# Chain steps in bursts and a preamble on one load queue: a change to a conv, DeltaNet and PEER block on one core

## The chip, the core and the metric

The kernel runs on one core of one Trainium2 chip. The core has a matrix engine (TensorE, PE in the rows; PEld is its weight load), three engines for elementwise work (VectorE, DVE; ScalarE, ACT; GpSimd, POOL), a queue that only issues transfers (SyncE, SP) and 16 DMA engines. Each engine runs its own instructions in the order in which they were written and waits for others by semaphores. The metric is the device time of one execution in microseconds, as the median of several runs.

## What is computed

One layer of a diffusion backbone over 256 latent and 256 context tokens of width 2048, in float32:

```python
mod  = split(silu(c)     @ w_mod + b_mod, 6)      # modulation of the latent tokens
modc = split(silu(c_ctx) @ w_mod + b_mod, 6)      # and of the context tokens
h  = rms_norm(x,   norm1_g) * (1 + mod[1])  + mod[0]
hc = rms_norm(ctx, norm1_g) * (1 + modc[1]) + modc[0]
y  = token_mixer(h, hc, ...)                      # one wide projection, then conv | gated DeltaNet
x  = x + mod[2] * y
h  = rms_norm(x, norm2_g) * (1 + mod[4]) + mod[3]
x  = x + mod[5] * peer(h, ...)                    # product keys, 16384 experts
return rms_norm(x, final_g)

# gated DeltaNet, for each of 16 heads, both directions, chunks of the 512 tokens:
#   q, k, v = l2norm/silu(short conv of 5 taps)
#   t_inv   = inverse(I + strict_lower(beta k k^T * decay))
#   scan:   v_new = u - w S;  o = (q e^g) S + attn v_new;  S = S e^g_last + k^T v_new
```

## The kernel before

The work falls into a **preamble** (to about 187 us in the trace), the **heads** (to about 1345 us) and the rest (convolution, output projections, experts), which the change doesn't touch. Instructions of every engine stand in the order in which the program writes them; no scheduler moves them.

**Products.** A weight tile of 128x2048 is loaded in two halves (`raw_load`, a ring of four buffers, all on SP's queue). `prep` splits a half into a high part `whi` (ACT, L201) and a rest `wlo` (POOL, in some places DVE, L205). `products` then runs 8 or 16 times `mm3`, which is three matmuls (L210 to L212): high by high, high by low, low by high. One `mm3` is called a product below. After each product `tick` advances a clock by one.

**Chain steps.** Everything else of a head is written as a generator that yields pauses in ticks, from the table `GAP`. `tick` runs all steps whose time has come, so their matmuls stand between two products. A head's four products are v, z (two heads late), k, q; after each follows `short_conv` (pauses C0 and C). `prepare` transposes v, k and q (pauses Pv, Pk, N), makes the Gram matrix G and A (PG, PA), and for each direction the decay matrix D, its product K with G, the high part kh, the block diagonal kb and the rest kl (PD, Pat, Pkh, Pkl). `invert` builds the inverse: a first X from kb (L706), four rounds of X and Y on compact 32-column tiles (LX, LY), then the expansion `Tf` of the result (L684) and two rounds on full tiles (F0, FX, FY, FZ), and a refinement with E, Z1, Z2. `scan` runs the recurrence over four chunks (Sv, Sr, Sn, SS, So2), normalises with So, and transposes the output (oT, Sa, Sg). PSUM banks: the products rotate through three (`psg`); the chains have two banks "d" and one each of "s", "p", "m".

**Modulation.** The first two of the six modulations are made in the preamble, in eight parts of 512 columns; a part takes eight tiles of 128x1024 (`mod_tile`, L296), a copy of the sums (`mod_row`, L312), and a transpose (`mod_columns`, L320). Between the tiles stand head 0's first products (`first_chunk`), as soon as the normalised tokens (`normed`) exist. Their sums of squares are made by `mean_squares` (ACT squares, DVE adds). Before, the tokens x and ctx are loaded in sixteen transfers that ACT issues, the modulation tiles by SP, seven in flight by three extra buffers (`mraw`). The other four modulations are made in the heads by `mods_rest`, one tile every 13 ticks.

## Time and profile before

| | us |
|---|---|
| median of 3 runs (3573.36 to 3578.66) | 3575.61 |
| the profiled execution | 3580.69 |
| its span in the profile | 3578.9 |
| PE busy | 3352.6 (94%) |
| DVE busy | 2193.8 (61%) |
| POOL busy | 1828.7 (51%) |
| ACT busy | 1485.2 (41%) |

The profile's page shows PE at nine tenths or more in most slices; the first slices and those of the heads are lower. Matmuls are pipelined, so a busy PE may still have bubbles; the distance from one start to the next tells more than a duration. A row of waits names the instruction that waited, the one that released it, the sum, the number of times and the longest.

### The profile page before, as it was taken

The numbers are of one execution on the slowest core, as the hardware profiler recorded it, in microseconds if no ns is written. First come the engines' busy times: TensorE is split into PE (matmuls) and PEld (weight loads), VectorE is DVE, ScalarE is ACT, GpSimd is POOL, SyncE is SP. The second block draws the span as 40 slices with busy tenths as digits, with TensorE's granted clock in tenths as the row PEclk, the third lists the DMA queues.
The fourth block names the chain that finished last, engine by engine and source line by source line (L and its number), as shares of the span: only waits on it lengthen the run. The fifth ranks groups of instructions, "written<-read, shape, count | busy, mean of one in ns | idle before, by whom it ended". The sixth has DMA issues, their size and how long they took to land. (4 is left out here: it accounts for less than half of the span.)

```text
span 3578.9 us, 71451 instructions
## 1 busy us (share of the span) xinstructions
PE 3352.6 (94%) x29428; PEld 3221.6 (90%) x29428; DVE 2193.8 (61%) x3963; ACT 1485.2 (41%) x2663; POOL 1828.7 (51%) x964
## 2 busy tenths in 40 slices
PE   5799999999998999999999899999999999999998
PEld 3588888888888889998999899999999999999998
DVE  3467666666667669986767999855333333333446
ACT  2234444444444444444433344544444444443443
POOL 1344434434445587777547544454454544444554
PEclk9799999999999999999999999999999999999999
DMA  8634433433432355554654456588556566665664
GB/s 308 215 119 131 127 120 120 128 125 122 131 108 81 108 181 184 183 183 153 218 183 164 144 169 211 180 318 290 195 194 196 193 194 195 194 194 191 211 210 162
DMA packets 177974, 629.26 MB, mean 176 GB/s; under 512 B 19056, under 2 KB 23792, under 8 KB 174576
## 3 DMA queue, kind: packets, MB, share of 16 engines
q1 hardware_dynamic: 174912, 618.98, 52.2%
q10 hardware_dynamic: 2736, 5.71, 0.4%
q8 instruction: 231, 3.78, 0.4%
q14 instruction: 95, 0.78, 0.1%
HBM read 601.42 MB, written 23.20 MB: 175 GB/s over the span
## 5 line engine op out<-in xcount | busy, mean ns | idle before, releaser
L205 POOL TENSOR_TENSOR wlo<-raw,whi 128x1024 fp32r<-128x1024 f32 x593 | 1447.2, 2442 | 1320.4 <-ACT whi L201 1250.2
L201 ACT CAST whi<-raw 128x1024 fp32r<-128x1024 f32 x896 | 936.6, 1048 | 1159.3 <-PE ps_p L211 779.8
L205 DVE TENSOR_TENSOR wlo<-raw,whi 128x1024 fp32r<-128x1024 f32 x303 | 429.8, 1418 | 767.0 <-ACT whi L201 764.0
L210 PE MATMUL ps_p<-hh,whi 128*128 128x256 f32 x2560 | 794.4, 310 | 11.6 <-DVE vT L559 9.1
L212 PE MATMUL ps_p<-hh,wlo 128*128 128x256 f32 x2560 | 734.6, 287 | 9.4 <-POOL wlo L205 9.3
L211 PE MATMUL ps_p<-hl,whi 128*128 128x256 f32 x2560 | 734.2, 287 | 0.0
L212 PE MATMUL ps_p<-h2h,wlo 128*128 128x256 f32 x2304 | 657.8, 286 | 18.7 <-DVE wlo L205 14.2
L210 PE MATMUL ps_p<-h2h,whi 128*128 128x256 f32 x2304 | 663.9, 288 | 3.1 <-ACT h2h L1311 1.6
L211 PE MATMUL ps_p<-h2l,whi 128*128 128x256 f32 x2304 | 656.4, 285 | 0.2 <-POOL h2l L1315 0.2
L212 PE MATMUL ps_p<-ph,wlo 128*128 128x256 f32 x2048 | 582.1, 284 | 7.2 <-POOL wlo L205 5.7
L211 PE MATMUL ps_p<-pl,whi 128*128 128x256 f32 x2048 | 580.9, 284 | 0.5 <-POOL pl L1492 0.5
L210 PE MATMUL ps_p<-ph,whi 128*128 128x256 f32 x2048 | 580.9, 284 | 0.0
L210 PEld LDWEIGHTS ps_p<-hh,whi 128*128 128x128 f32 x2560 | 499.8, 195 | 56.9 <-issue 53.7
L212 PEld LDWEIGHTS ps_p<-hh,wlo 128*128 128x128 f32 x2560 | 499.1, 195 | 11.7 <-POOL wlo L205 11.7
L211 PEld LDWEIGHTS ps_p<-hl,whi 128*128 128x128 f32 x2560 | 500.9, 196 | 0.9
L212 PEld LDWEIGHTS ps_p<-h2h,wlo 128*128 128x128 f32 x2304 | 446.1, 194 | 20.5 <-DVE wlo L205 15.4
L210 PEld LDWEIGHTS ps_p<-h2h,whi 128*128 128x128 f32 x2304 | 446.3, 194 | 3.8 <-ACT whi L201 1.9
L211 PEld LDWEIGHTS ps_p<-h2l,whi 128*128 128x128 f32 x2304 | 446.4, 194 | 0.5 <-POOL h2l L1315 0.5
L212 PEld LDWEIGHTS ps_p<-ph,wlo 128*128 128x128 f32 x2048 | 393.8, 192 | 9.9 <-POOL wlo L205 8.2
L211 PEld LDWEIGHTS ps_p<-pl,whi 128*128 128x128 f32 x2048 | 393.9, 192 | 0.7 <-POOL pl L1492 0.7
L210 PEld LDWEIGHTS ps_p<-ph,whi 128*128 128x128 f32 x2048 | 394.0, 192 | 0.2 <-issue 0.2
L911 DVE SCALAR_TENSOR_TENSOR ps_cv<-up,cw,ps_cv 128x256 f32<-128x256 f32 x464 | 226.8, 489 | 14.6
(323 smaller groups left out, 4961.7 us busy)
## 6 DMA issues: line engine op xcount, KB each, us to landing
raw<-in_w_in_dram SPq DMA_DIRECT2D x256, 512.0 KB, 4.2
raw<-in_peer_u_dram SPq DMA_DIRECT2D x256, 512.0 KB, 4.4
raw<-in_peer_v_dram SPq DMA_DIRECT2D x256, 512.0 KB, 4.5
raw<-in_w_mod_dram SPq DMA_DIRECT2D x96, 512.0 KB, 3.7
raw<-in_w_moda_dram SPq DMA_DIRECT2D x64, 512.0 KB, 5.5
raw<-in_w_dn_out_dram SPq DMA_DIRECT2D x32, 512.0 KB, 4.1
raw<-in_w_conv_out_dram SPq DMA_DIRECT2D x32, 512.0 KB, 4.6
raw<-in_w_out_dram SPq DMA_DIRECT2D x32, 512.0 KB, 4.2
```

The source lines that it names most:

```text
L201: nc.scalar.copy(hi, raw)
L205: eng.tensor_tensor(lo, raw, hi.bitcast(F32), ALU.subtract)
L210: nc.tensor.matmul(ps, wh, ah, start=start, stop=False)
L211: nc.tensor.matmul(ps, wh, al, start=False, stop=False)
L212: nc.tensor.matmul(ps, wl, ah, start=False, stop=stop)
L911: nc.vector.scalar_tensor_tensor(dst if i == CW - 1 else pr, up[n][:, :, i:i + GRID_W], cw[:, n, i:i + 1], pr, ALU.mult, ALU.add)
```

## The change

Two things. In the **preamble** the sixteen loads of x and ctx go to SP's queue, between the modulation tiles; the three extra buffers serve the first weights, which are loaded and split earlier; the constants are loaded in two pieces at the 53rd of 64 tiles into the ring of four, and copied after the seventh part; the second part's transpose comes at its sixth tile; the transposes use banks "d", and head 0's v product accumulates in bank "m", which leaves one `psg` bank free. In the **heads** `tick` runs due steps only at every third tick, the pauses are set anew, Tf is expanded in two instructions, and modulation tiles are taken in pairs at twice the pause.

```diff
-GAP = dict(N=10, C0=3, C=3.5, P0=0.5, Pv=3, Pk=4, Pn=2.5, PG=3, PA=3.5, PD=2.5, Pat=2, Pkh=2, Pkl=1, L0=4,
-           LX=4, LY=4.5, F0=7, FX=5, FY=5, FZ=2, IT=4.5, E=4, Z1=5, Z2=7, Sv=4, Sr=4, Sn=5, SS=6, So=12,
-           Sa=2, Sg=5, So2=3,
-           M=13, M0=2, DC=12, M1=16, MT=3, V=1.75, VA=2, VS=4.5, LN=4, NW=2, W=7, D=24, RT=5, RC=7, RB=11, ML=11, H0=21, HP=12, G0=4)
+GAP = dict(N=10, C0=0.5, C=3.5, P0=1.5, Pv=2.5, Pk=4, Pn=2.5, PG=3, PA=3.0, PD=2.5, Pat=2, Pkh=4.0, Pkl=1,
+           Pb=4, L0=4, LX=4, LY=4.0, F0=7, FX=5, FY=5, FZ=2, IT=6.5, E=4, Z1=5, Z2=5.0, Sv=4, Sr=5.0, Sn=5,
+           SS=5.0, So=10.5, Sa=0.5, Sg=6.5, So2=5.0, M=13.5, M0=2, DC=12, M1=16, MT=2.5, V=1.75, VA=2, VS=4.5,
+           LN=4, NW=2, W=7, D=24, RT=5, RC=7, RB=11, ML=11, H0=21, HP=12, G0=4)
...
     def tick():
         now[0] += 1
-        while todo and todo[0][0] <= now[0]:
-            step()
+        if now[0] % cur.get("burst", 1) == 0:
+            while todo and todo[0][0] <= now[0]:
+                step()
...
-        for c in range(0, NCH, 1024 // w):
-            mod_tile(ps, c, w, sc, following())
-            yield gap
+        for c in range(0, NCH, 2):
+            for k in range(2):
+                mod_tile(ps, c + k, w, sc, following.tiles.pop(0))
+            following(False)
+            yield 2 * gap
...
         for c in range(0, NCH, 2):
+            mod_load(1 if c < 14 else 0)
             for s, nm in enumerate(("ctxT", "xT")):
...
-                nc.scalar.dma_start(t, a[nm][:, c:c + 2, :])
+                nc.sync.dma_start(t, a[nm][:, c:c + 2, :])
...
-        cf = unit("cf").rearrange("p a b -> p (a b)")
-        nc.scalar.dma_start(cf, a["consts"])
...
                 x.at.append(at)
                 yield GAP['Pkl']
+            yield GAP['Pb']
...
-                nc.vector.tensor_tensor(o.rearrange("p c (b j) -> p c b j", j=32), bc(t, 2, [P, 8, 4, 32]),
-                                        bc(bd16.rearrange("p (b j) -> p b j", j=32), 1, [P, 8, 4, 32]), ALU.mult)
+                ov = o.rearrange("p c (b j) -> p c b j", j=32)
+                n = 4 if name == "Tf" else 8
+                for c in range(0, 8, n):
+                    nc.vector.tensor_tensor(ov[:, c:c + n], bc(t[:, c:c + n], 2, [P, n, 4, 32]),
+                                            bc(bd16.rearrange("p (b j) -> p b j", j=32), 1, [P, n, 4, 32]), ALU.mult)
...
-                if r == 1 and rows:
-                    mod_columns(*rows.pop(0), mod_bank)
+                if r == (5 if p == 1 else 1) and rows:
+                    mod_columns(*rows.pop(0), bank)
...
-                            pss = [psg.tile([P, len(seqs), T], F32, name="ps_p", tag="g") for _, seqs in first_jobs]
+                            pss = [mod_bank("ps_p").rearrange("p (s t) -> p s t", s=2)]
+                            pss += [psg.tile([P, len(seqs), T], F32, name="ps_p", tag="g") for _, seqs in first_jobs[1:]]
...
+                if k in (0, 1, 2, 20, 22, 24):
+                    load(len(raws) + 1)
+                if k in (11, 13, 15):
+                    prep()
+                if k == 52:
+                    cf = [raw_load(a["consts"][:, c:c + 1024], "cf") for c in (0, 1024)]
...
-            if p == 3:
+            if p == 6:
+                cur["side"] = None
                 early.close()
...
         start(mods_rest())
+        cur["burst"] = 3
         for h in range(1, nh):
```

At the program's start, PE before (ps_mod is a part's sums, x80 are ten tiles of eight matmuls, ps_modt its transpose, ps_tok and ps_rs belong to the norm):

```order
L296 MATMUL ps_mod<-raw,sc 32x128 x80
L320 MATMUL ps_modt<-cc,modrow 128x128
L296 MATMUL ps_mod<-raw,sc 32x128 x24
L339 MATMUL ps_tok<-cc,acc 128x1 x4
L296 MATMUL ps_mod<-raw,sc 32x128 x32
L352 MATMUL ps_rs<-dg,cc 128x128 x4
```

and PE after:

```order
L298 MATMUL ps_mod<-raw,sc 32x128 x80
L343 MATMUL ps_tok<-cc,acc 128x1 x4
L298 MATMUL ps_mod<-raw,sc 32x128 x32
L324 MATMUL ps_modt<-cc,modrow 128x128
L356 MATMUL ps_rs<-dg,cc 128x128 x4
```

The first transpose moved behind four more tiles, and the norm's first sums ahead of it.

At the same place, ACT before (the last loads of x and the constants, then the first square):

```order
L392 DMA x_120<-in_ctxT_dram 128x512
L392 DMA x_122<-in_xT_dram 128x512
L392 DMA x_124<-in_ctxT_dram 128x512
L392 DMA x_126<-in_xT_dram 128x512
L460 DMA cf<-in_consts_dram 128x2048
L419 ACTIVATE sq<-x_96 128x256
```

and ACT after:

```order
L271 DMA cc<-in_consts_dram 128x384
L383 ACT_TABLE_LOAD
L383 ACTIVATE cth<-pf 128x32
L420 ACTIVATE sq<-x_101 128x256
L420 ACTIVATE sq<-x_103 128x256
```

The squares now stand right behind the two small loads.

In a head, DVE around the expansion Tf before (ps_p is a short convolution's tap, Tc the compact inverse, c_749 constants; S, oacc and r belong to the scan of the head ahead):

```order
L834 SCALAR_TENSOR_TENSOR S<-S,egs,ps_S 128x128 x2
L848 SCALAR_TENSOR_TENSOR oacc<-ps_o,egs,oacc 128x128 x2
L554 SCALAR_TENSOR_TENSOR ps_p<-pad_763,pf,ps_p 128x512
L722 COPY_PREDICATED Tc<-lv,ps_Y 128x256
L684 TENSOR_TENSOR Tf<-Tc,c_749 128x1024
L690 STREAM_TRANSPOSE Tt<-Tc 128x256
L684 TENSOR_TENSOR Z<-Tt,c_749 128x1024
```

and DVE after:

```order
L830 SCALAR_TENSOR_TENSOR S<-S,egs,ps_S 128x128 x2
L546 SCALAR_TENSOR_TENSOR ps_p<-pad_1261,pf,ps_p 128x512
L718 COPY_PREDICATED Tc<-lv,ps_Y 128x256
L680 TENSOR_TENSOR Tf<-Tc,c_1246 128x512 x2
L686 STREAM_TRANSPOSE Tt<-Tc 128x256
L680 TENSOR_TENSOR Z<-Tt,c_1246 128x1024
L546 SCALAR_TENSOR_TENSOR ps_p<-pad_1261,pf,ps_p 128x512
L844 SCALAR_TENSOR_TENSOR oacc<-ps_o,egs,oacc 128x128 x2
```

Tf is two instructions, and the scan's oacc moved behind it.

In a head, PE at the Gram matrix before (ps_p are products; the step that follows is of the head ahead):

```order
L212 MATMUL ps_p<-hh_141,wlo 128x256
L637 MATMUL ps_G<-kT 128x128 x4
L210 MATMUL ps_p<-hh_140,whi 128x256
L211 MATMUL ps_p<-hl_144,whi 128x256
L212 MATMUL ps_p<-hh_140,wlo 128x256
L737 LDWEIGHTS E
```

and PE after:

```order
L212 MATMUL ps_p<-hh_153,wlo 128x256
L866 MATMUL ps_oT<-cc,oacc 128x128 x2
L629 MATMUL ps_G<-kT 128x128 x4
L210 MATMUL ps_p<-hh_151,whi 128x256
L211 MATMUL ps_p<-hl_155,whi 128x256
L212 MATMUL ps_p<-hh_151,wlo 128x256
L210 MATMUL ps_p<-hh_153,whi 128x256
L211 MATMUL ps_p<-hl_157,whi 128x256
L212 MATMUL ps_p<-hh_153,wlo 128x256
L210 MATMUL ps_p<-hh_152,whi 128x256
L211 MATMUL ps_p<-hl_156,whi 128x256
L212 MATMUL ps_p<-hh_152,wlo 128x256
```

Two steps of different heads now stand side by side, with three products behind them instead of one. Counted over the order of all heads, from the first transpose of v to the last oT, products are interrupted 614 times before and 420 times after.

## Rows read from the trace of the kernel before

**Rows 1.** Stages: stretch and length, busy us (instructions) by engine, clock, DMA share, GB/s.

```profile
0.00:187.00 187.00, 119.69 (x1477) 93.40 (x1478) 70.92 (x166) 45.45 (x98) 45.73 (x50) 0.86 0.71 253
187.00:1345.00 1158.00, 1058.56 (x10003) 965.12 (x10001) 795.14 (x1545) 493.25 (x1158) 562.62 (x346) 0.97 0.39 124
1345.00:3578.00 2233.00, 2174.32 (x17953) 2163.10 (x17951) 1327.76 (x2253) 946.50 (x1408) 1220.40 (x571) 0.99 0.59 196
```

**Rows 2.** PE's waits in the heads, 187 to 1345 us: total, times, longest.

```profile
PE ps_X L706 <- DVE kk L673: 29.0, 15, 3.5
PE ps_X L737 <- DVE Tf L684: 17.5, 13, 1.9
PE ps_qt L620 <- ACT kts L614: 8.1, 11, 0.8
PE ps_D L656 <- DVE De L669: 7.4, 8, 1.5
PE ps_vn L819 <- DVE r L810: 6.7, 12, 1.0
...
PE ps_o L841 <- DVE S L834: 4.5, 8, 1.7
```

**Rows 3.** PE's waits in the preamble, 0 to 187 us.

```profile
PE ps_modt L320 <- DVE modrow L312: 24.1, 3, 16.1
PE ps_mod L296 <- DMA raw<-in_w_moda_dram: 23.1, 22, 2.8
PE ps_p L210 <- DVE vT L559: 9.1, 1, 9.1
```

**Rows 4.** Timeline, 20 to 61 us: start, length, engine, instruction, idle before.

```profile
27.37 1.33 ACT L419 ACTIVATE sq<-x 128x256 f32<-128x256 f32 x4 [21.73 <-DMA x<-in_ctxT_dram]
...
41.17 0.28 DVE L312 COPY modrow<-ps_mod 128x128 f32<-128x128 f32 x1
...
41.51 0.48 PE L320 MATMUL ps_modt<-cc,modrow 128*128 128x128 f32 x1 [16.09 <-DVE modrow L312]
...
60.55 0.48 PE L320 MATMUL ps_modt<-cc,modrow 128*128 128x128 f32 x1 [7.56 <-DVE modrow L312]
```

**Rows 5.** Two stretches of the preamble; the last number is GB/s.

```profile
10.00:20.00 10.00, 5.67 (x88) 2.97 (x80) 0.00 (x0) 0.00 (x0) 0.00 (x0) 1.00 1.04 411
...
40.00:50.00 10.00, 7.73 (x107) 6.36 (x109) 4.08 (x9) 2.49 (x5) 0.18 (x1) 1.00 0.37 114
```

**Rows 6.** Timeline of PE right behind the wait for vT, 175 us.

```profile
175.14 0.42 PE L210 MATMUL ps_p<-hh,whi 128*128 128x256 f32 x1
175.35 0.42 PE L211 MATMUL ps_p<-hl,whi 128*128 128x256 f32 x1
```

**Rows 7.** Timelines of one head's Tf, 605 to 612 us: PE, then POOL, DVE, PE.

```profile
605.88 0.35 PE L721 MATMUL ps_Y<-Xc,Z 128*128 128x32 f16 x8
...
606.29 0.28 PE L211 MATMUL ps_p<-hl,whi 128*128 128x256 f32 x1
...
606.64 0.28 PE L211 MATMUL ps_p<-hl,whi 128*128 128x256 f32 x1
...
608.06 2.36 POOL L205 TENSOR_TENSOR wlo<-raw,whi 128x1024 fp32r<-128x1024 f32 x1 [3.10 <-ACT whi L201]
...
608.45 2.52 DVE L684 TENSOR_TENSOR Tf<-Tc,c 128x1024 f16<-128x1024 f16 x1
...
611.02 0.62 PE L737 MATMUL ps_X<-Tf,kk 128*128 128x128 f16 x8 [1.73 <-DVE Tf L684]
```

**Rows 8.** Tf in all heads (min/median/max ns), and POOL's wlo there (busy, mean ns).

```profile
L684 DVE TENSOR_TENSOR Tf<-Tc,c x16: 691/2528/2711, 229.8 to 1198.7; 128x1024 f16<-128x1024 f16 x16
...
L205 POOL TENSOR_TENSOR wlo<-raw,whi 128x1024 fp32r<-128x1024 f32 x165 | 396.3, 2402 | 447.4 <-ACT whi L201 417.1 <-PE ps_mod L296 24.3 <-PE ps_Z L737 5.6
```

**Rows 9.** A product's first two matmuls in the heads: busy us, mean ns.

```profile
L210 PE MATMUL ps_p<-hh,whi 128*128 128x256 f32 x1807 | 575.8, 319 | 1.3 <-ACT ut L894 1.3
L211 PE MATMUL ps_p<-hl,whi 128*128 128x256 f32 x1808 | 519.0, 287 | 0.0
```

More of the change, by code (lines that the diff above doesn't have):

```diff
@@ L147, in body, with raw_load @@
     todo, serial, now = [], itertools.count(), [0]
-    def raw_load(src, name="raw"):
-        raw = strm.tile([P, 1024], F32, name=name, tag="raw", bufs=RAW)
+    def raw_load(src, name="raw", pool=None):
+        raw = (pool or strm).tile([P, 1024], F32, name=name, tag="raw", bufs=3 if pool else RAW)
         if len(src.shape) == 3:
@@ L191, in load @@
             key, src = srcs[made[0]]
-            raws.append((key, raw_load(src)))
+            raws.append((key, raw_load(src, pool=cur.get("side"))))
             made[0] += 1
@@ L289, in following @@
             return tiles.pop(0) if take else None
+        following.tiles = tiles
         return following
@@ L383, in body @@
                                        chf.rearrange("p (c r) -> p c r", r=2), ALU.add, ALU.mult)
-        xs = [[], []]
-        for c in range(0, NCH, 2):
-            for s, nm in enumerate(("ctxT", "xT")):
-                tag = "kT" if c < 4 else "vT" if c < 6 else ("kk", "h2")[(c // 2 * 2 + s) % 2]
-                t = work([P, 2, T], tag=tag, name=f"x_{s}")
-                nc.scalar.dma_start(t, a[nm][:, c:c + 2, :])
-                xs[s] += [t[:, 0, :], t[:, 1, :]]
         def mod_bank(name):
@@ L398, in body @@
         early = ExitStack()
-        mraw = early.enter_context(tc.tile_pool(name="mraw", bufs=3))
+        cur["side"] = early.enter_context(tc.tile_pool(name="mraw", bufs=3))
         ahead, mod_seq = [], [(v, at // QTR, r) for v, at, _ in MODS for r in range(8)]
@@ L405, in mod_load @@
                 v, q, r = mod_seq.pop(0)
-                src, k = a["w_moda"][v, q, r], 63 - len(mod_seq)
-                if k < 32 and k % 7 in (4, 5, 6):
-                    raw = mraw.tile([P, 1024], F32, name="raw", tag="raw")
-                    nc.sync.dma_start(raw, src)
-                else:
-                    raw = raw_load(src)
-                ahead.append(raw.rearrange("p (j n) -> p j n", n=QTR))
+                raw = raw_load(a["w_moda"][v, q, r])
+                ahead.append(raw.rearrange("p (j n) -> p j n", n=QTR))
+        xs = [[], []]
+        for c in range(0, NCH, 2):
+            mod_load(1 if c < 14 else 0)
+            for s, nm in enumerate(("ctxT", "xT")):
+                tag = "kT" if c < 4 else "vT" if c < 6 else ("kk", "h2")[(c // 2 * 2 + s) % 2]
+                t = work([P, 2, T], tag=tag, name=f"x_{s}")
+                nc.sync.dma_start(t, a[nm][:, c:c + 2, :])
+                xs[s] += [t[:, 0, :], t[:, 1, :]]
         def mean_squares():
@@ L449, in body @@
         abl = [work([P, 8, 64], F32R, tag="al", name="abl") for _ in range(2)]
-        def first_weights():
-            yield from split_ab()
-            for _ in range(3):
-                load(1)
-                yield
-                prep()
-        cf = unit("cf").rearrange("p a b -> p (a b)")
-        nc.scalar.dma_start(cf, a["consts"])
         hh = [[unit(f"hh_{s}{u}", F32R) for u in range(2)] for s in range(2)]
-        hl = [[unit(f"hl_{s}{u}", F32R) for u in range(2 - s)] for s in range(2)]
+        hl = [[unit(f"hl_{s}{u}", F32R) for u in range(2)] for s in range(2)]
         def normed(c):
@@ L982, in take @@
                 assert ws[-1][0] == first_jobs[len(ws) - 1][0]
-        squares, weights = mean_squares(), first_weights()
+        squares, weights = mean_squares(), split_ab()
         n_q, n_c = D // QTR, QTR // P
         jobs, rows = iter(()), []
-        mod_load(6)
         for p, (v, at, w) in enumerate(MODS):
@@ L1002, in body @@
                         if q == 1:
-                            for _ in weights:
-                                pass
                             ps_ab = [bank("ps_ab0", "s"), bank("ps_ab1", "p")]
-                            pss = [psg.tile([P, len(seqs), T], F32, name="ps_p", tag="g") for _, seqs in first_jobs]
+                            pss = [mod_bank("ps_p").rearrange("p (s t) -> p s t", s=2)]
+                            pss += [psg.tile([P, len(seqs), T], F32, name="ps_p", tag="g") for _, seqs in first_jobs[1:]]
                             take(3)
@@ L1023, in body @@
                     take(1)
-                    if k == 50:
-                        load(2)
                 if k == 58:
@@ L1028, in body @@
                     load()
-                if r >= 4 or second:
+                if r >= 3 or second:
                     for _ in range(3):
@@ L1069, in body @@
                     pads.append(pd)
-                hl[1].append(unit("hl_11", F32R))
-        mod_columns(*rows.pop(0), mod_bank)
+        mod_columns(*rows.pop(0), bank)
         scales(n_q - 1)
@@ L1100, in body @@
         drain()
+        cur["burst"] = 1
         pa.close()
```

21 lines of the change are left out of this document (10 added, 11 removed).

## The prediction

> **What bounds the kernel now.** I read the stages first. TensorE (PE) is busy 1058.6 of the 1158 us from 187 to 1345 us (the heads) and 2174.3 of the 2233 us behind them, but only 119.7 of the first 187 us (the preamble) [rows 1]. The diff leaves everything behind 1345 us as it is, so those 2234 us stand; what can move is 67 us of idle PE in the preamble and 99 us in the heads, and the way in which PE alternates between products and chain steps.
>
> Next, who ended the idle time in the heads [rows 2]. Most of it (73 us in the six rows) is a chain step (a small matmul of the DeltaNet) that PE reaches before VectorE (DVE) or ScalarE (ACT) has made its operand: 29.0 us for kb (15 times of 16 heads), 17.5 us for Tf (13 times), 8.1 us for kts. So the pauses, not an engine's load, set this loss.
>
> In the preamble three things end it [rows 3]: a transposed modulation row (24.1 us in 3 waits), modulation tiles from HBM (23.1 us in 22 waits) and one wait of 9.1 us for head 0's v. The timeline shows the first [rows 4]: ACT issues the sixteen loads of x itself and starts squaring at 27.37 us only; DVE adds up the squares, the copy of the modulation row stands behind the additions (41.17 us), PE gets its transpose at 41.51 us after 16.09 us of idleness, and that of the next part at 60.55 us after 7.56 us. Meanwhile the load buffers are full and the transfers starve: 411 GB/s from 10 to 20 us, 114 GB/s from 40 to 50 us [rows 5].
>
> **The change, part by part. Preamble.** (a) The loads of x leave ACT's queue for SP's, so ACT squares each tile as it lands; the first transpose stands behind the sixth tile of the second part, not the second. What is late next is the stream itself. Up to the second transpose it needs 17 modulation tiles of 0.52 MB, 4.2 MB of x, 2.1 MB of first weights and ab columns, 0.5 MB of parameters: 15.7 MB, 38 us at 411 GB/s, 40 with the start; I take 45 us instead of 60.55, as the rate is not always reached: 15 us off, bounds 18 and 8. Every dma_start on SP is queued in order: the fifth and later modulation tiles wait there for a buffer that PE frees, and loads of x stand behind them, which is why I don't take 20. (b) The side pool of three buffers now holds the first weights, so modulation tiles have four buffers instead of seven in the first half. Part of the 23 us of waits for tiles can grow: 2 us back, bounds 0 and 8. (c) The 1 MB of constants is loaded late, in the busy stream, and holds two of the four buffers until they are copied: 2.6 us at 411 GB/s; 3 back, bounds 0 and 6. (d) The first weights, loaded earlier, are at nothing: their loads and splits stand beside waits for tiles, whose bounds hold them. (e) Head 0's v product takes a spare PSUM bank, so that head 1's first product needn't wait 9.1 us for vT [rows 3]; the matmuls after that wait run at about 0.21 us apart [rows 6] where the normal distance is 0.12 [rows 7], some 1.5 us more. What is late next: the first modulation tile of the heads wants that spare bank 16 products (6 us) later, and vT stood 9.1 us away, so up to 3 us come back. 8 us off, bounds 10.6 and 4. (f) The transposes of the modulation rows move into the two PSUM banks of the accumulators, so each part's first tile waits for DVE's copy of the row before, 0.28 us [rows 4], seven times: at nothing behind the waits for tiles, 2 us without them. Sum for the preamble: 15 - 2 - 3 + 8 = 18 us off.
>
> **Loads on one queue, by the page.** The Trainium skill, "DMA: Bandwidth & Descriptors", section "Issuing engines are not separate DMA queues", says that issuing from several engines only saves issue time, since all run on the same engines. By that alone part (a) would move nothing, the sum would be 55 us and the time 3520, which is close to rival 2 below; the trace shows no rate that differs by queue, but an ACT that is held up in its own order.
>
> **Heads: the pauses.** One product is three matmuls, 0.35 us (606.29 to 606.64) [rows 7], or 0.36 at 0.12 each. Chain steps that are due now run at every third product only, 1.1 us apart plus the chain's own matmuls.
> - kb: the X step stood one product behind kb's line. Now four more are added, and two more ahead of kb in each direction. At 0.12 us a product matmul the order has 5.4 to 6.8 us of PE work between the second D and X, against 3.1 to 4.7. The wait averaged 1.9 us; 27 of 29 us go, bounds 29 and 10.
> - Tf: the timeline of one head tells it [rows 7]. VectorE's Tf starts at 608.45, 0.39 us after GpSimd's (POOL's) wlo at 608.06, and lasts 2.52 us, to when wlo ends and half a microsecond more; PE waits 1.73 us. Over the sixteen heads Tf is 0.69 us at least and 2.53 in the median, and a wlo lasts 2.40 [rows 8]. So it is a collision, and it recurs because every head stands alike. wlo starts 1.8 us after the last matmul of a weight half (606.29); in the old order the fourth Y ends one product before that point. In the new order it stands three products and four chain matmuls before it, about 1.7 us, and the half before ended 5.6 us earlier: its wlo is over. Tf fits between. 15 of 17.5 us go, bounds 17.5 and a loss of 10.
> - With Tf goes what stood behind it on DVE, r (6.7 us): 5 off, bounds 7 and 0. The De wait (7.4) has two products more: 7 off. S (4.5) has two more behind So2: 4 off. Together bounds 18 and 0.
> - What comes: kts has the same pause of four, but in bursts mostly three products and a chain step, so its 8.1 us become about 12: 4 back. The last transpose, oT, has 11 products of pause behind the squares, not 14, and stands in one burst with G: 6 back, bounds 0 and 25. Steps at three products where there were four or five (the S to kS links above all): 4 back, since the order gives most of them over a microsecond and the waits on them so far are below 2 us each, bounds 0 and 30.
>
> Sum: 27 + 15 + 5 + 7 + 4 - 4 - 6 - 4 = 44 us off. The smaller waits stand.
>
> **Heads: the switches.** The first matmul of a product behind chain steps is longer: L210 averages 319 ns, L211 287 [rows 9], 32 ns over 1807 products, 58 us. The order has 614 interruptions of the products before and 420 now; 58/614 is 94 ns each, 194 fewer give 18 us at most, and nothing if the matmul ahead of a switch is as much shorter. I take 8. Modulation tiles in pairs are in that count; they load two ahead as before, and 27 products of pause per pair are 13.5 per tile, against 13: six parts take 1,326 products, which the 1,700 of the heads hold.
>
> **A port, by the page.** The Trainium skill, "SBUF — State Buffer", section "Who interferes with whom", says that a DVE instruction with two SBUF inputs and a GpSimd instruction that reads SBUF use one shared interface, and whichever comes second blocks fully until the first has ended. The trace agrees (2.53 against 0.69 us). The rule also speaks against the split of Tf into two: POOL can take the port between the halves, and the second would then cost a whole wlo more; where the order puts Tf clear of wlo, that doesn't arise.
>
> **Sum.** 18 + 44 + 8 = 70 us off the profiled execution's 3580.69 us gives 3510.7. That execution lies 5.1 us above the median of the three runs (3575.61), so 3505.6 by the median; I say 3505.
>
> **Rivals.**
> 1. The collisions only move. z, oacc and the expansion of Z are two-input or SBUF-only DVE instructions too, and each can fall into the 2.4 us of a wlo. If one per head does, with the 1.3 us that Tf cost PE, 16 heads give 21 us back; if two do, 42, and the heads' gain of 44 is gone. For it: 165 wlo fill 396 of the heads' 1158 us [rows 8]. Against: the order gives most links more than a microsecond to spare. 3505 + 21 to 42, say 3535.
> 2. The preamble yields only (e), since the stream from HBM is the bound anyway: what (a) to (d) give together, 15 - 2 - 3 = 10 us, doesn't come, 3515. For it: 23 us of waits for tiles [rows 3]. Against: 16 us of idle PE while the rate was a quarter of its best [rows 4, 5].
> 3. Steps starve in bursts, and the kernel is slower. A burst gives DVE the work of several chains at once, and the next burst comes 1.1 us of products later. If the operand of each burst's first step is late by d, 420 bursts cost 420 d. It decides at 70/420 = 0.17 us beyond what is in the sum: at 0.3 us, 3505 + 126 = 3631. For it: DVE is busy 795 of 1158 us [rows 1]. Against: between bursts lie also the chains' own matmuls, and 1158 us less the gain over 420 bursts are 2.6 us from one to the next.
> 4. Waits vanish altogether: all 99 us, 18 of switches, 25 of the preamble: 3434 by the median. For it: kb, Tf and De are half of the idle time and regular. Against: kts and oT remain.
>
> **How the numbers follow.** A run of this kernel can be told from no change at about 0.2%, 7 us. My forecast (3480 to 3525) has 0.50; rival 1 0.18; rival 2 0.10; rival 3 0.08; rival 4, taken as anything below 3480, 0.09; and 0.05 for gains and losses that cancel within 7 us. Faster: 0.50 + 0.17 + 0.10 + 0.09 = 0.86; same 0.01 of rival 1 and the 0.05, 0.06; slower 0.08. Range 3455 to 3555: it takes in rivals 1 and 2 and the upper part of rival 4, and leaves out rival 3, the 0.05 and the rest of rival 4.
>
> **What would show it.** Right: PE's first idle stretch of 16 us gone and ACT's first square before 12 us; no 9 us wait at head 1; Tf's two halves at some 0.4 us each; no wait for kb above 10 us in total; mean L210 below 310 ns. Wrong: other DVE rows at 2 us and more next to wlo, waits of oT or kS above 20 us, PE idle in the heads above 80 us. My weakest step is the total of the waits that come new, for which the old trace has only rows with other pauses.

## The result and the profile after

The changed kernel takes 3496.95 us (median of 4 runs, 3494.38 to 3501.31) against 3577.14 us for the kernel before on the same chip (3573.36 to 3580.14): ratio 0.9774, 95% interval 0.9762 to 0.9786, 80.2 us or 2.3% faster. The forecast was 3505 us with a range of 3455 to 3555. The profiled execution took 3494.38 us, its span is 3492.6 us; that is 86.3 us below the profiled execution of before. One execution each of e6, e11 and e12 below took 4518, 3975 and 12433 us; these three stand in none of the numbers.

The stages of the changed kernel, with the same columns as [rows 1]:

```profile
0.00:165.00 165.00, 110.46 (x1397) 82.17 (x1398) 61.44 (x140) 37.69 (x84) 40.35 (x47) 0.87 0.78 276
165.00:1265.00 1100.00, 1029.99 (x10087) 960.13 (x10086) 777.49 (x1590) 508.94 (x1171) 570.42 (x349) 0.99 0.40 132
1265.00:3492.00 2227.00, 2173.12 (x17948) 2161.44 (x17947) 1319.46 (x2252) 947.53 (x1408) 1221.04 (x570) 0.99 0.59 197
```

The heads are still PE's, and their granted clock is 0.99, where it was 0.97. (The granted clock is the share of TensorE's full 2.4 GHz that it got; at the lower of its two levels, 1.2 GHz, a row shows 0.50.) Stage borders don't part the same work in both kernels, so I compare by work: the 1440 products from the 201st to the 1641st first matmul of L210, which fill most of the heads. In this view of a stretch the first number after the length is PE's busy time, and the third from the end the granted clock. First before, then after:

```profile
243.82:1227.34 983.52, 896.65 (x8625) 811.28 (x8622) 682.73 (x1358) 417.03 (x1009) 440.27 (x272) 0.97 0.37 117
```

```profile
238.93:1145.67 906.74, 856.92 (x8640) 795.20 (x8639) 655.89 (x1371) 425.50 (x1011) 441.74 (x272) 1.00 0.39 127
```

The stretch is 76.8 us shorter: 37.1 us less idle time (983.52 - 896.65 = 86.9 against 49.8) and 39.7 us less busy time for nearly the same matmuls (8625 and 8640 in the rows). The stretch also starts 4.9 us earlier, which is all that the preamble gave, and at its end the lead (by how much earlier the same product starts than before) is 81.7 us. At the last product of L210 it is 80.5. The other 5.8 us of the 86.3 come behind it, in work that the change leaves as it is; there e1 gains 2.0 us on the kernel before, e2 loses 0.8 and e8 3.4, and no run shows why.

PE's waits in the heads of the changed kernel, 165 to 1265 us, to be held against [rows 2] (total, times, longest):

```profile
PE ps_kS L803 <- DVE oacc L844: 13.3, 13, 1.2
PE ps_vn L815 <- ACT vb L792: 7.8, 8, 1.4
PE ps_qt L612 <- ACT kts L606: 7.4, 13, 0.6
PE ps_oT L866 <- DVE oacc L861: 6.5, 3, 3.8
PE ps_D L648 <- DVE As L640: 5.1, 10, 0.8
...
PE ps_X L702 <- DVE kk L665: 2.0, 2, 1.0
...
PE ps_vn L815 <- DVE r L806: 0.7, 1, 0.7
```

The two rows that led before, kb with 29.0 and Tf with 17.5 us, are 2.0 and nothing. In their place stand one for the scan's oacc (L844, 13.3), one for vb (7.8) and one for As (5.1), with waits of about a microsecond or less. Tf and the expansion of Z in all heads, against [rows 8] (minimum, median, maximum in ns):

```profile
L680 DVE TENSOR_TENSOR Z<-Tt,c x80: 691/693/2754, 210.9 to 1122.5; 128x1024 f16<-128x1024 f16 x80
L680 DVE TENSOR_TENSOR Tf<-Tc,c x32: 410/422/825, 229.6 to 1121.7; 128x512 f16<-128x512 f16 x32
```

A half of Tf takes 0.42 us in the median, 0.83 at most. Tf does not stand clear of wlo, though. In 11 of the 16 heads its first half starts in the last half microsecond of one and takes 0.81 to 0.83 us. One such head, POOL, DVE and PE:

```profile
577.61 2.37 POOL L205 TENSOR_TENSOR wlo<-raw,whi 128x1024 fp32r<-128x1024 f32 x1 [2.91 <-ACT whi L201]
579.46 1.14 DVE L680 TENSOR_TENSOR Tf<-Tc,c 128x512 f16<-128x512 f16 x2
583.89 0.61 PE L733 MATMUL ps_X<-Tf,kk 128*128 128x128 f16 x8
```

What changed is its place between its neighbours: in 13 heads Tf started 2.4 us behind the fourth Y and 2.6 to 2.8 us ahead of PE's X before; now it starts 0.67 us behind Y and 4.0 to 4.5 us ahead of X. By these distances even a Tf of 2.5 us would be ready in time.

And a product's first two matmuls, against [rows 9]:

```profile
L210 PE MATMUL ps_p<-hh,whi 128*128 128x256 f32 x1829 | 557.1, 305 | 1.3 <-ACT ut L890 1.3
L211 PE MATMUL ps_p<-hl,whi 128*128 128x256 f32 x1829 | 518.3, 283 | 0.0
```

Both means fell, the second one too (287 to 283), though nothing interrupts that one. Something made all matmuls shorter, and that is the clock. The kernel before shows how it falls, in four stretches around one wait for kb; the granted clock is the third number from the end:

```profile
444.00:450.50 6.50, 6.37 (x53) 5.23 (x45) 4.98 (x8) 5.14 (x13) 5.93 (x3) 1.00 0.53 161
450.50:452.50 2.00, 0.01 (x1) 0.00 (x0) 1.32 (x4) 1.28 (x5) 0.39 (x2) 1.00 0.43 86
452.60:455.80 3.20, 3.20 (x21) 2.28 (x21) 2.42 (x5) 0.69 (x3) 0.94 (x1) 0.50 0.26 102
456.00:462.00 6.00, 6.00 (x68) 5.86 (x69) 3.02 (x7) 1.78 (x4) 0.00 (x0) 1.00 0.27 90
```

PE idles for 2.07 us, and right behind that it runs at 1.2 GHz (0.50) until about 456 us. It is "busy" all the while, but a product's matmuls there stand 0.21 us apart instead of 0.12, so the wait costs PE time a second time, as busy time. By the trace's record of the clock the stretch of 1440 products has 14 such falls before, 51.2 us at the lower clock, and one after, 3.4 us. Each fall of before begins near the end of a wait of 1.6 us or more, or up to 2 us behind it: ten waits for kb, two for Tf, one for Gs and one for the scaled oacc ahead of oT. Not every such wait draws one: the stretch has 24 of them.

With that the 76.8 us part into three: idle time 37.1; clock 23.4 (half of the time that PE was busy at the lower clock: 25.1 against 1.7); and 16.4 us less busy time at full clock, for nearly the same matmuls with fewer interruptions. The half is an upper estimate: it takes every matmul to last twice as long at the lower clock, while a product's matmuls stand 0.213 us apart instead of 0.119, by which 0.44 of the time is lost. By that share the clock is 20.8 us and the rest 18.9. The table below uses the half throughout.

The preamble, against [rows 3]:

```profile
PE ps_mod L298 <- DMA raw<-in_w_moda_dram: 37.8, 29, 5.4
PE ps_mod L298 <- DVE sc L386: 6.9, 1, 6.9
PE ps_p L210 <- ACT whi L201: 5.4, 1, 5.4
PE ps_p L212 <- POOL wlo L205: 1.6, 1, 1.6
PE ps_modt L324 <- DVE modrow L316: 1.4, 2, 1.0
```

and its timeline at five places, against [rows 4] (the last bracket is the idle time before):

```profile
7.70 0.42 ACT L420 ACTIVATE sq<-x 128x256 f32<-128x256 f32 x1 [1.86 <-DMA x<-in_ctxT_dram]
```

```profile
49.30 0.33 PE L324 MATMUL ps_modt<-cc,modrow 128*128 128x128 f32 x1 [0.96 <-DVE modrow L316]
```

```profile
118.69 0.58 PE L210 MATMUL ps_p<-hh,whi 128*128 128x256 f32 x1 [5.37 <-ACT whi L201]
```

```profile
139.96 2.31 PE L298 MATMUL ps_mod<-raw,sc 128*32 128x128 f32 x32 [5.40 <-DMA raw<-in_w_moda_dram]
```

```profile
176.19 1.08 PE L298 MATMUL ps_mod<-raw,sc 128*32 128x256 f32 x8 [3.77 <-DMA raw<-in_w_mod_dram]
```

The 24.1 us behind modulation rows are 1.4, the squares start at 7.70 instead of 27.37 us, the second transpose stands at 49.30 instead of 60.55, and the first product starts 10.6 us earlier. (The second transpose stands behind 18 of the 64 tiles in both kernels; the one that moved behind four more tiles is the first, that of the first part's sums.) But then the lead melts. From the second transpose to the last one of the preamble the changed kernel takes 9.9 us longer: PE waits 18.7 us for tiles there instead of 14.5, and 5.37 instead of 1.2 us for the whi of a first weight. That cast stands on ACT behind the casts of the normalised tokens, which come behind the sixth part's transpose (108.39 us), so it goes at the pace of the tiles as well. (In the whole preamble the waits for tiles grow from 23.1 to 37.8 us; the other 10.5 lie ahead of the second transpose.) The longest wait for a tile, 5.40 us, is the one behind the constants, and the last transpose of the preamble stands at 147.11 us, 1.4 earlier than before. Head 1 then gains the 9 us of vT and the slow matmuls behind that wait [rows 6]: its lead is 12.7 us behind them. It gives 6.4 us back at the heads' first two modulation tiles, of which 5.3 are waits (3.77 at 176.19 and one of 1.54), and 1.0 in the next three products, which run at the lower clock, 0.64 us each.

### The profile page after: what moved, and what is told of

The parts are those of the page before. It is cut to its first block, busy times and chain, and to the rows that moved or that the text cites. A ratio compares the mean times of both kernels' runs of the same rounds, so it can differ in the third digit from the quotient of the medians.

```text
span 3492.6 us, 71481 instructions
## 1 busy us (share of the span) xinstructions
PE 3313.6 (95%) x29428; PEld 3203.7 (92%) x29428; DVE 2158.4 (62%) x3980; ACT 1494.2 (43%) x2663; POOL 1831.8 (52%) x964
## 4 chain that ended last, share of the span: by engine, by line
PE 53%; DVE 5%; POOL 2%; issue 2%; ACT 1%; DMA 1%; SPq 0%; ACTq 0%; POOLq 0%; DVEq 0%
PE ps_p L212 17%; PE ps_p L210 17%; PE ps_p L211 17%; PE ps_W L1444 2%; POOL wlo L205 2%; DVE wlo L205 1%; ACT whi L201 1%; DMA raw<-in_peer_v_dram 0%; DMA rawg<-in_w_mod_dram 0%; DVE i L1335 0%; DVE sc L1336 0%; DVE i L1338 0%; DVE cand L1363 0%; POOL pl L1491 0%; DVE v L1337 0%
## 5 line engine op out<-in xcount | busy, mean ns | idle before, releaser
L210 PE MATMUL ps_p<-hh,whi 128*128 128x256 f32 x2560 | 768.0, 300 | 6.7 <-ACT whi L201 5.4
L211 PE MATMUL ps_p<-hl,whi 128*128 128x256 f32 x2560 | 726.5, 284 | 0.0
L210 PE MATMUL ps_p<-h2h,whi 128*128 128x256 f32 x2304 | 662.1, 287 | 3.4 <-ACT whi L201 1.8
L210 PE MATMUL ps_p<-ph,whi 128*128 128x256 f32 x2048 | 580.6, 283 | 1.4 <-ACT yT L1498 0.6
L210 PEld LDWEIGHTS ps_p<-hh,whi 128*128 128x128 f32 x2560 | 492.9, 193 | 23.9 <-issue 15.7
L212 PEld LDWEIGHTS ps_p<-hh,wlo 128*128 128x128 f32 x2560 | 491.9, 192 | 12.7 <-POOL wlo L205 12.7
L211 PEld LDWEIGHTS ps_p<-hl,whi 128*128 128x128 f32 x2560 | 493.2, 193 | 0.8
L212 PEld LDWEIGHTS ps_p<-h2h,wlo 128*128 128x128 f32 x2304 | 445.0, 193 | 13.5 <-DVE wlo L205 8.0
L210 PEld LDWEIGHTS ps_p<-h2h,whi 128*128 128x128 f32 x2304 | 445.1, 193 | 3.9 <-ACT whi L201 2.0
L212 PEld LDWEIGHTS ps_p<-ph,wlo 128*128 128x128 f32 x2048 | 393.7, 192 | 11.1 <-POOL wlo L205 9.3
L210 PEld LDWEIGHTS ps_p<-ph,whi 128*128 128x128 f32 x2048 | 393.9, 192 | 2.2 <-issue 0.9
```

The costliest lines, as they stand in the source:

```text
L210: nc.tensor.matmul(ps, wh, ah, start=start, stop=False)
L211: nc.tensor.matmul(ps, wh, al, start=False, stop=False)
L212: nc.tensor.matmul(ps, wl, ah, start=False, stop=stop)
```

## The experiments

All kernels compute the whole output; e8 adds matmuls of no use. The table has the median, the ratio to the kernel before with its interval, and for the same 1440 products of one profiled execution the wall time, PE's idle time, the falls of the clock with what they cost, and the busy time at full clock. They ran in groups of four, each beside its own runs of the kernel before; the ratio is what compares them. The last three columns are worked out from each trace as above: wall less the union of PE's matmuls is idle, half of PE's busy time at the lower clock is what the falls cost (an upper estimate, as said), and the rest is busy time at full clock. Rows of waits in this section are of 200 to 1230 us.

| kernel | median us | ratio | wall | idle | falls, us | busy |
|---|---|---|---|---|---|---|
| before | 3577.1 | 1 | 983.5 | 86.9 | 14, 25.1 | 871.6 |
| changed | 3497.0 | 0.9774 [0.9762, 0.9786] | 906.7 | 49.8 | 1, 1.7 | 855.2 |
| e1 preamble alone | 3561.8 | 0.9955 [0.9940, 0.9970] | 973.0 | 87.5 | 7, 11.6 | 873.8 |
| e2 heads alone | 3506.3 | 0.9799 [0.9780, 0.9818] | 909.0 | 49.5 | 2, 4.6 | 854.9 |
| e3 no bursts | 3514.6 | 0.9829 [0.9810, 0.9848] | 918.3 | 53.5 | 1, 1.7 | 863.1 |
| e4 old pauses | 3628.0 | 1.0137 [1.0115, 1.0159] | 1039.3 | 129.4 | 25, 51.0 | 858.9 |
| e5 kb's pauses back | 3548.7 | 0.9918 [0.9901, 0.9934] | 961.4 | 87.2 | 10, 18.5 | 855.7 |
| e6 Tf whole | 3500.3 | 0.9773 [0.9749, 0.9796] | 906.4 | 48.5 | 1, 2.8 | 855.0 |
| e7 constants later | 3494.4 | 0.9771 [0.9754, 0.9787] | 909.3 | 49.6 | 2, 4.7 | 854.9 |
| e8 filler, on before | 3568.5 | 0.9972 [0.9961, 0.9983] | 968.1 | 69.9 | 2, 3.4 | 894.9 |
| e9 single tiles | 3503.1 | 0.9793 [0.9777, 0.9809] | 912.4 | 42.8 | 2, 3.4 | 866.2 |
| e10 x on ACT | 3502.7 | 0.9787 [0.9773, 0.9801] | 907.2 | 49.6 | 1, 2.5 | 855.1 |
| e11 scan's pause | 3496.5 | 0.9765 [0.9750, 0.9780] | 903.4 | 44.7 | 2, 4.0 | 854.7 |
| e12 three pauses more | 3589.0 | 1.0026 [1.0015, 1.0038] | 1001.2 | 115.9 | 14, 24.9 | 860.5 |

**Which half: e1 and e2.** 

```
e1:  changed kernel, but GAP, tick, mod_part, expand and prepare of before
e2:  kernel before, but GAP, tick, mod_part, expand and prepare of the change
```

> The preamble's part of the change alone, with the heads' pauses, steps, Tf and modulation tiles as before. Theory (the lead of the preamble is lost again before the heads: the first product comes 10.6 us earlier in the changed kernel, the last modulation tile 1.4, the products behind head 1's first ten about 4.5): 3572 us, 5 below the kernel before, and TensorE idle in the heads about 99 us as before. Rival (the preamble's 18 us of the prediction do come, and something of the heads takes 13 of them in the changed kernel): 3559 us.

> The heads' part alone (pauses, bursts of three, Tf in two, modulation tiles in pairs) on the preamble of before. Theory (the heads give 76 us whatever stands ahead of them): 3501 us, 4 above the changed kernel, waits for kb below 5 us and a granted clock of 0.99 in the heads where the kernel before has 0.97. Rival (the preamble's place for head 0's v and its loads give the heads their lead): 3515 us or more, with new waits in the first heads.

The heads alone give 70.8 us (3577.05 to 3506.26), most of the 80, as expected. The preamble alone gives 15.2 us, where I expected 5, and comes near the rival. Its trace says that this is only half a gain of the preamble: at the 201st product its lead is 6.8 us. The rest grows in the heads, though their order and their idle time are those of before (87.5 us): the clock fell 7 times there instead of 14. It has 24 waits of 1.6 us or more there, as the kernel before. So the same waits do not always draw a fall, and the time of a kernel with many such waits has a share that its order doesn't decide. It is no accident of one trace: the granted clock of whole executions is 0.982 in the mean of e1's seven and 0.979 in the ten of before. Why 17 of the 24 drew none here stays open. The two gains add up to 86 us, more than the 80 of both together, since each counts falls that the other takes away too (13.5 and 20.5 us of the 23.4, by the column of falls).

**Bursts against pauses: e3 and e4.**

```
e3:  cur["burst"] = 3   ->  cur["burst"] = 1
e4:  GAP = dict(...)    ->  GAP of before; no yield of Pb
```

> The changed kernel with its new pauses, but chain steps at any product again. Theory (the pauses remove the waits and keep the clock, the bursts pay for the switches only: 41 us less busy time in the heads, of which the clock is about 20): 3515 us, some 20 above the changed kernel; first matmuls of a product at 315 ns and more, second ones unchanged, the clock 0.99, TensorE's waits in the heads below 75 us. Rival 1 (the bursts also keep links apart, and without them the waits come back): 3540 us or more, waits of 90 us and more. Rival 2 (the switches cost nothing, since the matmul ahead of a switch is as much shorter): 3497 us.

> The changed kernel with the pauses of before, steps still at every third product. Theory (the pauses are worth the waits for kb and the clock behind them, the bursts the switches): 3545 us, some 50 above the changed kernel, with 15 waits for kb of about 2 us each back and a granted clock of 0.97 to 0.98 in the heads. Rival (the rounding up to three products is itself what lengthens the pauses): 3515 us or less, waits for kb below 10 us in total.

Without bursts the kernel is 17.6 us slower than the changed one by the medians, as the theory had it. In the 1440 products idle time is 3.7 us more, the clock stays, and busy time grows by 7.9 us, for 522 interruptions of the products instead of 386 (58 ns each). That is 11.6 us; the rest lies outside the stretch and was not followed. With bursts and the old pauses it is 51 us slower than before, and both expectations fell: I had 3545 and 3515, it took 3628. The bursts are no small help that adds to the pauses; without the new pauses they lose. What they lose in, as groups of DVE instructions in the stretch of the 1440 products (busy us, mean ns):

```profile
L679 DVE TENSOR_TENSOR Z<-Tt,c 128x1024 f16<-128x1024 f16 x75 | 96.7, 1290 | 2.6
L860 DVE TENSOR_SCALAR oacc<-oacc,sm 128x128 f32<-128x128 f32 x30 | 48.2, 1706 | 0.0
...
L679 DVE TENSOR_TENSOR Tf<-Tc,c 128x512 f16<-128x512 f16 x30 | 39.9, 1368 | 0.5
```

These are the SBUF-only instructions, at 1.3 to 1.7 us in the mean where undisturbed ones take 0.69, 0.34 and 0.42. Over all heads 43 of 80 Z and 18 of 32 halves of Tf ran beside a wlo of 2.4 us, and 31 of 32 oacc beside a wlo or an Lg, another two-input instruction of POOL (1.05 us). The waits are PE's for kb (31.3 us, 14 times), r (27.1) and kts (14.4):

```profile
PE ps_X L701 <- DVE kk L665: 31.3, 14, 4.9
PE ps_vn L814 <- DVE r L805: 27.1, 12, 2.6
PE ps_qt L612 <- ACT kts L606: 14.4, 14, 1.1
```

On top of 42.5 us more idle time than before come 11 falls more of the clock, 25.9 us. The Trainium skill, "SBUF — State Buffer", section "Who interferes with whom", names both forms: two-input instructions, and `tensor_scalar` in the modes that take both ports; the row on oacc agrees with the second.

**kb's pauses back: e5.**

```
Pkh=4.0, Pb=4   ->   Pkh=2, Pb=0
```

> The changed kernel with kb's pauses as before (no four products behind kb, two instead of four ahead of it), bursts kept. Theory (a long wait costs twice: TensorE's idle time, and a lower granted clock some 14 us behind it): the waits for kb are back at 25 to 30 us over the heads, the clock falls behind most of those of 2 us and more, 5 to 12 falls with 8 to 20 us lost, 3497 + 27 + 14 = 3538 us. Rival (the falls of the clock come from something else that the change took away): 3497 + 27 = 3524 us with one fall, as in the changed kernel.

It takes 3548.7 us, 52 more than the changed kernel and 10 more than the theory said. Idle time rises by 37.4 us and the clock falls 10 times instead of once, 16.8 us. The waits stand at other steps than expected, one step behind kb:

```profile
PE ps_X L711 <- DVE Tc L705: 21.9, 16, 2.0
PE ps_kS L803 <- DVE oacc L844: 13.9, 14, 1.4
PE ps_X L702 <- DVE kk L665: 10.4, 10, 1.3
```

kb itself costs 10.4, and the compact inverse that follows it on DVE 21.9. So these pauses pay for the whole start of the inverse. The stretch is 54.7 us longer for 37.4 us of idle time, 1.46 us for each. The rival, one fall as in the changed kernel, is out.

**The clock by itself: e8.** In the kernel before, ahead of the first X step of each head:

```
 px = compact("ps_X")
+for _ in range(12):
+    nc.tensor.matmul(px, id16, bc(ic16, 1, C8), start=True, stop=True)
```

> The kernel before, with twelve matmuls of no use (128x256 each, overwritten by the step itself) ahead of each inverse's first X step, so that TensorE works in some 1.4 us of each wait for kb; nothing else is moved. Theory (the clock falls behind long idle stretches of TensorE): the wait itself is only filled, but most of the falls in the heads go, from 13 (47.8 us at the lower clock) to 4 or fewer, and the time falls by 12 to 20 us: 3560 us. Rival 1 (the falls have another cause): 13 falls and 3577 us. Rival 2 (matmuls of no use delay kb's operands or the heads behind): 3580 us and more.

The wait that is shown above (452.58 us) looks so in this kernel, and the clock of the stretch behind it:

```profile
453.19 1.47 PE L706 MATMUL ps_X<-c 128*128 128x256 f16 x12
454.50 0.26 PE L708 MATMUL ps_X<-c,kk 128*128 128x32 f16 x4
455.51 0.26 PE L708 MATMUL ps_X<-c,kk 128*128 128x32 f16 x4 [0.76 <-DVE kk L673]
455.62 0.36 PE L210 MATMUL ps_p<-hh,whi 128*128 128x256 f32 x1
```

```profile
455.00:458.20 3.20, 2.69 (x33) 2.10 (x33) 2.92 (x6) 1.23 (x5) 1.40 (x1) 1.00 0.39 141
```

kb is no earlier, PE waits for it as before, but works meanwhile; the clock stays at 1.00. Over the stretch 2 falls are left of 14, the clock costs 3.4 us instead of 25.1, and 1440 products take 15.4 us less although PE has more to do: 15 rows of fillers, 1.31 us each, are 19.7 us. Idle time is 17.0 us less and all busy time only 1.6 more, so the clock gave back 18.0 us for 12 falls, where the halves of the table say 21.7. By the medians it is 11.1 us faster than before (interval of the ratio 0.9961 to 0.9983), a little less than the 12 to 20 expected; 2.1 us are lost ahead of the stretch, where fillers stand too. The granted clock is 0.981 to 0.985 in all ten executions, and 0.976 to 0.982 in the thirteen of before. Neither rival holds: work of no use makes this kernel faster, because the idle stretches cost the clock.

**Tf's split: e6.** `n = 8` for Tf.

> The changed kernel with Tf in one DVE instruction. Theory (Tf's place ahead of wlo is what removes the collision, not its split): Tf at about 0.7 us in most heads, 3497 us within 4. Rival 1 (the split frees DVE for something between or shortens what wlo can hit): 2.5 us again in a third of the heads and more, 3505 to 3515 us. Rival 2 (the split costs, and the page's port falls to POOL between the halves): 3490 us, 2 to 7 faster.

3500.3 us, ratio 0.9773 against 0.9774: no difference, and neither rival came. Tf in one piece takes 1.07 us in the median, the two halves together about as much; 2.5 us doesn't come back:

```profile
L680 DVE TENSOR_TENSOR Tf<-Tc,c x16: 691/1073/1083, 229.4 to 1120.4; 128x1024 f16<-128x1024 f16 x16
```

It is 1.07 and not 0.69 because Tf starts in the last half microsecond of a wlo here too, in 11 of 16 heads. The split does nothing; Tf's place is the gain.

**Modulation tiles in pairs: e9.** mod_part one tile at a time, `yield gap` behind each.

> The changed kernel with the heads' modulation tiles one at a time again (13.5 products of pause for each). Theory (each interruption of the products costs some 0.1 us of busy time; there are up to 48 more): 3497 + 3 to 6 = 3501 us, idle time and clock as in the changed kernel. Rival (the pair costs nothing and gains nothing, the gain in busy time is all in the chain's bursts): 3497 us.

3503.1 us, 6 more than the changed kernel, ratio 0.9793 against 0.9774; the intervals overlap. The total is the theory's, its parts are not: at full clock 11.0 us more busy time, 7.0 us less idle, one fall more, and only 9 interruptions more in the stretch (395 against 386) where I had counted up to 48. Some 6 of the 11 us are the tiles themselves: alone, a tile's eight matmuls take 0.57 us to the next product, a pair takes 1.00 us, and the stretch has 44 pairs. The other 5 were not followed. So of busy time the pairs give 11 and the bursts 8 us (e3), which is 19 together and fits the 18.9 that are left when the clock is 20.8. Single tiles also save head 1 the wait for its second tile.

**The preamble's terms: e7 and e10.**

```
e7:  if k == 52: cf = ...   ->   if k == 57; copies after the last part
e10: nc.sync.dma_start(t, a[nm][...])   ->   nc.scalar.dma_start(...)
```

> The changed kernel with the 1 MB of constants loaded behind the last modulation tile instead of ahead of four of them, and copied after the last part. Theory (the constants in the busy stream cost the lead of the preamble between 131 and 147 us, 5.4 us of wait for one tile): the last modulation tile 4 us earlier, at about 142 us, and 3493 us. Rival (the stream or the heads' first modulation tiles take it back): 3497 us, with the wait moved behind 147 us.

> The changed kernel with the loads of x on ACT's queue again, nothing else moved. Theory (from 70 us on the preamble goes at the pace of the modulation tiles and their buffers, so a later start of the norm is made up again): first product up to 10 us later, the last modulation tile within 2 us, 3497 to 3500 us. Rival 1 (the prediction's term: the queue is worth 15 us of the preamble, all the way to the heads): 3508 us and more. Rival 2 (SP's queue, with x out of the way, brings modulation tiles sooner): 3490 us.

With the constants behind the last tile, the last transpose of the preamble comes 3.8 us earlier, and 2.1 us of that are there at the 201st product:

```profile
143.28 0.48 PE L324 MATMUL ps_modt<-cc,modrow 128*128 128x128 f32 x1 [0.41 <-DVE modrow L316]
```

The median is 2.5 us lower; the ratio (0.9771 against 0.9774) can't tell that from nothing. With x on ACT's queue, ACT squares from 21.33 us on, the second transpose stands at 51.90 us, 2.6 later, the first product comes 2.8 later, the 201st 3.1, and the median is 5.7 us higher (ratio 0.9787 against 0.9774; the intervals overlap). The queue of x is worth some 3 us here, neither the 15 of the prediction nor nothing, and of the 11.3 us at the second transpose it gives 2.6; the rest is the new order, which no run parts further.

**More pauses: e11 and e12.** On e7:

```
e11: yield GAP['SS']   ->   yield GAP['SS'] + (3 if n == 2 else 0)
e12: e11 with Pk=6, Sv=6, PA=4.5   (4, 4, 3.0)
```

> The changed kernel with the constants behind the last modulation tile, as in the run before, and three more products of pause between the third and the fourth scan step, where TensorE waits 13.3 us in 13 waits for the last oacc of the step ahead. Theory (the bank of the scan is free a burst later at most): 12 of the 13.3 us go, 3494 - 12 = 3482 us. Rival (the scan then falls differently against wlo and Z, and other waits come): 3490 to 3500 us, with new waits of 5 us and more for r, S or oT.

> The run before with three pauses more: two products behind the transposes of k (TensorE waits 7.4 us for kts), two ahead of the scan's first step (7.8 for vb) and 1.5 behind As (5.1). Theory (pauses remove waits one by one, at no cost): 3482 - 15 = 3467 us. Rival (each shift moves the head's later steps against wlo, and waits come as large as those that go): 3480 to 3500 us.

e11 takes away the wait for oacc, and 10.3 us for X, 6.3 for r and 4.4 for wlo come; 4.9 us of idle time are saved instead of 12, and its ratio is the changed kernel's within the interval, as the rival had it. e12 is 92.5 us slower than e11, outside both the theory and the rival. Its waits and the expansion of Z:

```profile
PE ps_Y L717 <- DVE Xc L713: 28.8, 22, 2.2
PE ps_X L733 <- ACT Z L747: 26.9, 15, 2.2
PE ps_oT L866 <- DVE oacc L861: 19.9, 14, 3.0
```

```profile
L680 DVE TENSOR_TENSOR Z<-Tt,c x80: 691/2396/2862, 210.7 to 1215.1; 128x1024 f16<-128x1024 f16 x80
```

Z takes 2.40 us in the median instead of 0.69. The timelines of POOL and DVE in one head show where it went:

```profile
475.45 2.34 POOL L205 TENSOR_TENSOR wlo<-raw,whi 128x1024 fp32r<-128x1024 f32 x1 [3.48 <-ACT whi L201]
```

```profile
475.86 2.48 DVE L680 TENSOR_TENSOR Z<-Tt,c 128x1024 f16<-128x1024 f16 x1
```

Two more pauses of two products and one of one and a half have moved the inverse onto wlo, as Tf was in the kernel before [rows 7]: 60 of the 80 Z run beside one, 14 in the changed kernel. Idle time rises by 71 us, and the clock costs 20.9 more.

## Why the prediction was right, and where it was not

The total came out 8 us from the median, but by errors that cancel.

**Preamble, 18 us forecast, 4.9 found** (6.8 in e1). (a) was right at the place to which I worked it out: no idle time of 16 us, squares before 12 us, the second transpose 11 us earlier, within the bounds of 8 to 18. The step that failed is that I carried this gain to the end of the preamble. Behind that transpose lie another 46 modulation tiles, and up to the last transpose the kernel loses 9.9 us: 4.2 more of waits for tiles and 4.2 more for a whi that the tiles hold up. (b) and (c) had 5 together; the constants of (c) alone are 3.8 in e7. So (a) to (d) give 1.4 us, not 10. (e) was right in what goes and too small in what comes back: 7.4 us around the heads' first two modulation tiles, not 3. The mechanism of rival 2, that the stream is the bound anyway, is what happened, and what is left, 4.9 us, is less than the 8 that rival 2 left to (e).

**The rule on queues.** By the sentence of the Trainium skill that the prediction cites ("DMA: Bandwidth & Descriptors", "Issuing engines are not separate DMA queues") the queue of x would move nothing but issue time; I had 15 us for (a). e10 measures some 3 us at the 201st product and shows that ACT's own order made the late squares (21.33 us against 7.70). The measurement lies nearer to the rule of the Trainium skill.

**Pauses, 44 us forecast, 37.1 found.** kb lost exactly the 27 us (29.0 to 2.0), Tf all of its 17.5 against 15, De its 7.4, r 6.0 of 6.7, S its 4.5. For Tf the reading was right in its sign only: I had the wlo of the half before as over, and in 11 heads Tf still starts within it; by the rows the wait went because Tf starts 1.7 us earlier behind its Y and X comes 4.0 us or more behind its start. kts did not grow (7.4 against 12), nor did oT (6.5 against 6.3). The mis-sized term is the steps at three products: 4 us, bounds 0 and 30. The three rows that came new (oacc, vb, As) are 26 us.

**Switches, 8 us forecast, 16.4 found** (18.9 by the share of 0.44). For the bursts the 8 was right: e3 has 58 ns for each interruption, between the forecast's 94 and nothing, though the middle was a choice without a row. The mis-sized part is the pairs. The prediction has them as interruptions in its count; by e9 they are worth 11 us at 9 interruptions.

**The clock, nothing forecast, 23.4 us found** (20.8 by the share of 0.44). The whole term was missing. [rows 1] showed 0.97 in the heads. (e) does price the slower matmuls at one place, behind the wait for vT [rows 6], but the waits in the heads got no such price. The stretch right behind a kb wait would have shown the level of 0.50, and that 2 us of idle time cost more than 2 us.

So 4.9 + 37.1 + 16.4 + 23.4 = 81.8 at the end of the stretch, against 70. The number came out right because what was missing at the clock and the switches (32 us) outweighs what was too much in the preamble and the pauses (20) by little.

**Rivals.** Rival 3 (steps starve in bursts) did not happen, but e4 shows that it was one table away: 3628 us, against the 3631 that I gave it. I priced its deciding point at 0.17 us a burst; in e4 idle time and clock are 68 us over some 400 bursts, 0.17 us, and without the new pauses nothing stands on the other side but 13 us of busy time. Rival 1 (collisions move to Z, oacc) did not happen in the changed kernel (14 of 80 Z beside a wlo, a median of 0.69 us), and is what makes e4 and e12 slow. Against it I had put that most links have more than a microsecond to spare; that does not protect, since a collision costs 1.7 us. Rival 4 (all waits vanish) is out: 49.8 us of idle time remain in the stretch.

**The signs.** All that were named for right came: no idle stretch of 16 us, squares from 7.70 us on, no 9 us at head 1, halves of Tf at 0.42 us, kb at 2.0 us in total, L210 at 305 ns. Those for wrong did not: the wait for kS is 13.3 us, PE idles 70 us in the heads (1100.00 less 1029.99), and a Z at 2.7 us is an exception with a median of 0.69. But no sign was named for the clock, and none for the preamble behind its first third.

## What to carry over

Where one engine's order repeats in every round, a collision of 2 us recurs in every round or in none, so pauses have to be judged as a set by the traces of whole rounds: a few products of pause removed 37 us of idle time here and brought 71 there (e12). Price an idle stretch of the matmul engine with the clock behind it, and look at the granted clock right behind the longest waits before you call a wait cheap. And follow a gain at the start of a stream-bound stage to the stage's end, not to the first place where it shows.

## What the hardware showed that I had not expected

In a stage that is over 90% busy, the granted clock fell to 0.50 14 times in the stretch before, each time near the end of a wait of 1.6 to 3.5 us or up to 2 us behind it. The falls cost some 20 to 25 us, and twelve small matmuls in the waits for kb left 2 of the 14 (e8). Of 24 such waits 14 drew a fall in one kernel and 7 in another whose heads have the same order (e1), so such a kernel's time varies with more than its order: 3569.7 to 3583.9 us over the ten runs of before beside e1 to e4. And DVE's scaling of oacc, 128x128 with one tensor from SBUF, is lengthened by a two-input instruction of POOL as DVE's two-input instructions are: 1.71 us in the mean in e4, where 31 of 32 had one beside them, and 0.34 in the median in e12, where 29 of 32 had none.
